# A transposed input that comes out of TensorE already normalised, in the first layer of a two-block transformer

## The chip, the cores and the metric

The kernel runs on one core of one Trainium2 chip. The metric is the device time of one execution in microseconds (us). Before the change it is 1310.2 us, the median of three runs (1309.93 to 1312.19). Lower is better.

## The reference, cut to what matters

Two transformer blocks run one behind the other on an input `x` of 256 tokens by 1024 features, in float32. The first block has a gated delta-net layer and a block-attention layer, each with an MLP. The second has four mixing branches, a cross-attention and a gated feed-forward. The change lies in the first few steps of the first layer:

```python
def rmsnorm(x, g):
    xf = x.astype(jnp.float32)
    y = xf * lax.rsqrt(jnp.mean(xf * xf, axis=-1, keepdims=True) + RMS_EPS)
    return (y * g.astype(jnp.float32)).astype(x.dtype)

def gated_deltanet(hn, w_in, ...):          # hn = rmsnorm(x, mix_norm_g[0])
    proj = hn @ w_in                         # q, k, v, z and 16 gate columns
    qkv = jax.nn.silu(causal_depthwise_conv(proj[..., :3 * DN_DIM], conv_w))
    ...
    beta = jax.nn.sigmoid(b_raw)             # from the gate columns
    g = -jnp.exp(a_log) * jax.nn.softplus(a_raw + dt_bias)
    o = chunk_gated_delta_rule(q, k, v, g, beta)   # needs a triangular solve
    ...

h = x
h = h + gated_deltanet(rmsnorm(h, mix_norm_g[0]), ...)
```

## The kernel before, in words

Everything is held transposed: features on the 128 partitions, the 256 tokens along the row. `x` is a tile of 8 such blocks, one for each 128 features. A float32 product is made from three products of half-precise parts. `split` writes a tile's high part on ScalarE and its low part on VectorE. The high and low parts of the normalised input are `xh` and `xl`, those of a weight `wh` and `wl`, and `mm3` adds the three products that matter. A weight comes from HBM in pieces of 512 KB (`wr`), fetched on SyncE's queue, four pieces deep.

The order of the instructions on each engine is set when the program is built, by a list scheduler that works from priorities (`high_priority`, `later`) and from `after`, which holds instructions back behind others. On the chip each engine works through its list in order and waits on semaphores.

The first layer goes as follows.

- `load_x` fetches `x` as two halves of 128 tokens (`xt`), transposes them on TensorE into four PSUM banks, and squares and sums the tokens on ScalarE (`token_rs`). That gives 1/rms of each token (`xrs`), put on a diagonal (`xdg`). A product of ones with the diagonals spreads 1/rms along a PSUM row (`p`).
- The transposed banks are copied to `x`. `normed` multiplies `x` by gain and row into a scratch tile `nrm` on VectorE, two blocks at a time, and splits it.
- `gates` makes the 16 gate columns (`ba`, transposed to `bat`) and from them `beta` and the log decay `gt`, through a string of tiny instructions (`sl_u` and the like). It needs two short rows from HBM, `alog` and `dtb`. `ea`, the exponential of `alog`, is the first to read one of them.
- `decays` turns `gt` into four decay tiles `m`. `project` makes k, q and v, a group of 512 columns at a time. Each group is 96 products of 128 columns into the two PSUM banks called `acc`. ScalarE empties them into `pad` and `cy`, VectorE adds three taps (12 instructions `cy` for a group), and ScalarE applies SiLU.
- `unit_keys` and `gram` give the matrices `A`. They travel through HBM (`ga`, `at`), and 31 steps of VectorE (`tmp`, `zt`) solve them. The result travels through HBM again (`gz`, `Z`), and TensorE goes on from `Z` ("Z stage" below). All 768 products of the eight groups (q, k and v, and the output gate `z`) stand ahead of the Z stage in TensorE's list.

## Time and profile before

| | |
|---|---|
| median of three runs | 1310.2 us |
| the profiled execution | 1310.08 us |
| its span in the trace | 1308.3 us |
| TensorE busy | 1261.0 us, 96% |
| VectorE busy | 867.1 us, 66% |
| ScalarE busy | 737.8 us, 56% |
| mean granted TensorE clock | 0.977 of full speed |

The span is the time between the first and the last instruction that the profiler saw. The profiled execution is 1.78 us longer than its span. A busy share is a mean over stages with different limits, so the start of the kernel has to be read by itself.

### The profile page before, as it was taken

The numbers are of one execution on the slowest core, as the hardware profiler recorded it, in microseconds if no ns is written. First come the engines' busy times: TensorE is split into PE (matmuls) and PEld (weight loads), VectorE is DVE, ScalarE is ACT, GpSimd is POOL, SyncE is SP. The second block draws the span as 40 slices with busy tenths as digits, with TensorE's granted clock in tenths as the row PEclk, the third lists the DMA queues.
The fourth block names the chain that finished last, engine by engine and source line by source line (L and its number), as shares of the span: only waits on it lengthen the run. The fifth ranks groups of instructions, "written<-read, shape, count | busy, mean of one in ns | idle before, by whom it ended". The sixth has DMA issues, their size and how long they took to land.

```text
span 1308.3 us, 23770 instructions
## 1 busy us (share of the span) xinstructions
PE 1261.0 (96%) x9674; PEld 1199.7 (92%) x9674; DVE 867.1 (66%) x1385; ACT 737.8 (56%) x1124; POOL 20.9 (2%) x68
## 2 busy tenths in 40 slices
PE   7997789999999999999999999999999998999998
PEld 6997688999999999999999987899999997999997
DVE  5799236644547666744546997998556685877775
ACT  5874536645546445755545644675447565656554
POOL 2010100000000000000000000000000000000000
PEclk8998689999999999999999999999999999999999
DMA  6454303666664744656652653446664654465652
GB/s 199 143 171 145 81 1 129 219 196 187 183 182 141 216 153 143 210 166 181 188 166 64 194 162 87 139 131 192 183 188 148 208 161 129 132 205 170 184 177 84
DMA packets 99633, 207.32 MB, mean 158 GB/s; under 512 B 9694, under 2 KB 12292, under 8 KB 99524
## 3 DMA queue, kind: packets, MB, share of 16 engines
q1 hardware_dynamic: 98114, 202.85, 50.7%
q0 software_dynamic: 928, 2.88, 0.8%
q8 instruction: 76, 1.25, 0.4%
q14 instruction: 33, 0.27, 0.1%
q10 hardware_dynamic: 482, 0.08, 0.0%
HBM read 204.21 MB, written 1.57 MB: 157 GB/s over the span
## 4 chain that ended last, share of the span: by engine, by line
PE 86%; DVE 6%; ACT 3%; issue 2%; DMA 2%; POOL 0%; DVEq 0%; SPq 0%; ACTq 0%; POOLq 0%
PE acc L53 53%; PE ps L53 32%; DVE wl L56 1%; ACT wh L76 1%; PE ps L603 1%; DVE cy L59 1%; DVE tmp L56 1%; PE ps L893 0%; DVE zt L56 0%; DVE sq L56 0%; DMA wr<-in_w_xkv_dram 0%; DMA xt<-in_x_dram 0%; DMA Z<-gz 0%; DMA gz<-zt 0%; DVE mx L879 0%
## 5 line engine op out<-in xcount | busy, mean ns | idle before, releaser
L56 DVE TENSOR_TENSOR wl<-wr,wh 128x1024 fp32r<-128x1024 f32 (+1 forms) x384 | 465.6, 1217 | 308.2 <-ACT wh L76 307.3
L76 ACT ACTIVATE wh<-wr 128x1024 fp32r<-128x1024 f32 (+1 forms) x384 | 402.3, 1052 | 394.3 <-PE acc L53 246.9
L53 PE MATMUL acc<-xh,wh 128*128 128x256 f32 (+1 forms) x1064 | 305.9, 288 | 7.8 <-DVE z L59 5.1
L53 PE MATMUL acc<-xh,wl 128*128 128x256 f32 (+1 forms) x1064 | 303.8, 286 | 3.5 <-DVE wl L56 3.5
L53 PE MATMUL acc<-xl,wh 128*128 128x256 f32 (+1 forms) x1064 | 304.4, 286 | 0.8 <-DVE xl L56 0.8
L53 PE MATMUL ps<-xh,wh 128*128 128x256 f32 (+1 forms) x872 | 248.5, 285 | 6.7 <-ACT xh L69 3.5
L53 PE MATMUL ps<-xl,wh 128*128 128x256 f32 (+1 forms) x872 | 248.2, 285 | 0.5 <-DVE xl L56 0.3
L53 PE MATMUL ps<-xh,wl 128*128 128x256 f32 (+1 forms) x872 | 248.0, 284 | 0.0
L53 PEld LDWEIGHTS acc<-xh,wh 128*128 128x128 f32 (+1 forms) x1064 | 204.4, 192 | 11.4 <-issue 6.5
L53 PEld LDWEIGHTS acc<-xh,wl 128*128 128x128 f32 (+1 forms) x1064 | 204.1, 192 | 6.0 <-DVE wl L56 3.7
L53 PEld LDWEIGHTS acc<-xl,wh 128*128 128x128 f32 (+1 forms) x1064 | 204.6, 192 | 3.2 <-issue 1.5
L53 PEld LDWEIGHTS ps<-xh,wh 128*128 128x128 f32 (+1 forms) x872 | 166.8, 191 | 8.4 <-ACT xh L69 3.9
L53 PEld LDWEIGHTS ps<-xl,wh 128*128 128x128 f32 (+1 forms) x872 | 166.9, 191 | 1.6 <-DVE xl L56 1.1
L53 PEld LDWEIGHTS ps<-xh,wl 128*128 128x128 f32 (+1 forms) x872 | 167.0, 192 | 0.3
L53 PE MATMUL acc<-hh,wh 128*128 128x256 f32 x512 | 144.6, 282 | 0.0
L53 PE MATMUL acc<-hh,wl 128*128 128x256 f32 x512 | 144.3, 282 | 0.0
L53 PE MATMUL acc<-hl,wh 128*128 128x256 f32 x512 | 144.2, 282 | 0.0
L53 PEld LDWEIGHTS acc<-hh,wl 128*128 128x128 f32 x512 | 97.3, 190 | 0.0
L53 PEld LDWEIGHTS acc<-hh,wh 128*128 128x128 f32 x512 | 97.2, 190 | 0.0
L53 PEld LDWEIGHTS acc<-hl,wh 128*128 128x128 f32 x512 | 97.1, 190 | 0.0
L59 DVE SCALAR_TENSOR_TENSOR yc<-cpad,vec_b,yc 128x256 f32<-128x256 f32 x120 | 51.6, 475 | 0.1
L59 DVE SCALAR_TENSOR_TENSOR fy<-pad,vec_b,fy 128x256 f32<-128x256 f32 x88 | 36.9, 478 | 0.1
(418 smaller groups left out, 1759.6 us busy)
## 6 DMA issues: line engine op xcount, KB each, us to landing
wr<-in_mlp_w_up_dram SPq DMA_DIRECT2D x64, 512.0 KB
wr<-in_mlp_w_down_dram SPq DMA_DIRECT2D x64, 512.0 KB
wr<-in_w_in_dram SPq DMA_DIRECT2D x44, 512.0 KB
wr<-in_w_up_dram SPq DMA_DIRECT2D x44, 512.0 KB
wr<-in_dn_w_in_dram SPq DMA_DIRECT2D x32, 512.0 KB
wr<-in_w_gate_dram SPq DMA_DIRECT2D x32, 512.0 KB
wr<-in_mb_w_in_dram SPq DMA_DIRECT2D x24, 512.0 KB
wr<-in_w_down_dram SPq DMA_DIRECT2D x22, 512.0 KB
```

Source lines behind the costliest of these rows:

```text
L53: return self.nc.tensor.matmul(out, lhsT=lhsT, rhs=rhs, start=start, stop=stop, skip_group_check=True)
L56: return (eng or self.nc.vector).tensor_tensor(out=out, in0=a, in1=b, op=op)
L59: self.nc.vector.scalar_tensor_tensor(out, a, s, b, op0=op0, op1=op1, **kw)
L76: a = self.nc.scalar.activation(hi, src, AF.Copy)
L603: nc.tensor.transpose(p[:, i * P:(i + 1) * P], zz[:, i, :], self.ident)
```

## The change

Both halves of `x` are now squared in two parts, one on VectorE (`stt` with a sum) and one on ScalarE. The diagonal of 1/rms is the right-hand operand of the products that transpose `xt`, so that the four PSUM banks hold the input transposed and normalised. `scaled` takes the high part (ScalarE) and the low part (VectorE) straight from PSUM, with the gain as the scale, one block of 256 at a time. `nrm` and the row `p` are gone. Eleven products of ones with themselves stand at TensorE's start in place of six. The plain transposes that `x` itself needs (it is added to the layer's output much later) come 200 priority steps later, out of `transposed_in`, with four copies on ScalarE. The first three 512 KB pieces of the weight are fetched ahead of the piece with the gate columns, which was first.

```diff
@@ load_x
-                banks = [self.ps() for _ in range(4)]
-                for i in range(6):
-                    self.mm(banks[i % 4][:, 0:P], self.ones, self.ones, True, True)
-                for c in range(2):
-                    for k in range(KD):
-                        o = (k % 2) * T + c * P
-                        tr = nc.tensor.transpose(banks[k // 2][:, o:o + P], xt[:, c, k * P:(k + 1) * P], self.ident)
-                dg = self.token_rs(xp, xt, "x", xp.tile([P, 2, D], F32, name="xsq"))
-                p = self.ps()
-                for c in range(2):
-                    row = self.mm(p[:, c * P:(c + 1) * P], self.ones, dg[:, c, :], True, True)
-                cp = nc.vector.tensor_copy(x[:, 0:2, :], self.pairs(banks[0]))
+                warm = self.ps()
+                for i in range(11):
+                    self.mm(warm[:, 0:P], self.ones, self.ones, True, True)
...
+                for c in range(2):
+                    if c:
+                        sq_after.enter_context(self.after(self.last_exp))
+                    u, v = ss[:, 2 * c:2 * c + 1], ss[:, 2 * c + 1:2 * c + 2]
+                    self.stt(sq[:, c, 0:half], xt[:, c, 0:half], 1.0, xt[:, c, 0:half], OP.mult, OP.mult, accum_out=u)
+                    self.act(sq[:, c, half:D], xt[:, c, half:D], AF.Square, accum_out=v)
+                    self.ts(u, u, 1.0 / D, EPS, OP.mult, OP.add)
+                    self.rsqrt_wide(rs[:, c:c + 1], v, D, u)
+                    last = self.ts(dg[:, c, :], self.ident, rs[:, c:c + 1], None, OP.mult)
...
+                for c in range(2):
+                    for k in range(KD):
+                        o = (k % 2) * T + c * P
+                        tr = self.mm(banks[k // 2][:, o:o + P], xt[:, c, k * P:(k + 1) * P], dg[:, c, :], True, True)
+                last = self.last_vec, self.last_exp, last
+                for i in range(4):
+                    with self.after(*last):
+                        if i < 3:
+                            self.ahead(W, 2 * i, 2, 1024, 512)
+                            last = self.last_split
+                        if i == 2:
+                            self.ahead(W, 0, 8, 4096, 16)
+                    o = self.pairs(banks[i])
+                    with self.after(*last):
+                        for j in range(2):
+                            last = self.scaled(xg, 2 * i + j, o[:, j, :], g[:, 2 * i + j:2 * i + j + 1])
+            with self.later(200), self.after(tr):
+                self.transposed_in(xt, None, lambda k, o: self.copy(x[:, k:k + 2, :], o))
-            with self.tc.high_priority():
-                for k in range(2, KD, 2):
-                    sc = self.copy(x[:, k:k + 2, :], self.pairs(banks[k // 2]))
-            last = sc, cp
-            for i in range(4):
-                with self.after(*last):
-                    last = self.normed(xp, xg, x, g, p[:, 0:T], range(2 * i, 2 * i + 2))
-                with self.after(*last):
-                    if i < 3:
-                        self.ahead(W, *((0, 8, 4096, 16) if i == 0 else (2 * i - 2, 2, 1024, 512)))
```

The scheduler then places many later instructions elsewhere. Three places matter. The first is the start of TensorE's list. `ps` and `acc` are PSUM banks, and `16x256` marks the gate columns. Before:

```order
L53 MATMUL ps<-tri 128x128 x6
L399 MATMUL ps<-ident,xt 128x128 x16
L53 MATMUL ps<-xdg,tri 128x128
L178 MATMUL ps<-ident,vrow_a_143 128x128
L178 MATMUL ps<-ident,vrow_a_144 128x9
L53 MATMUL ps<-xdg,tri 128x128
L53 MATMUL ps<-xh,wh 16x256
```

After the change:

```order
L53 MATMUL ps<-tri 128x128 x11
L177 MATMUL ps<-ident,vrow_a_113 128x128
L177 MATMUL ps<-ident,vrow_a_114 128x9
L53 MATMUL ps<-xdg,xt 128x128 x16
L53 MATMUL acc<-xh,wh 128x256
```

The gate columns no longer come first: their 24 products stand behind the 96 of the first k group. Further on, the products of `gt` (`decays`) stand behind 164 of the 768 `acc` products where they stood behind 116, and the last products of `gram` behind 286 where they stood behind 317. The plain transposes are spread through the first 170.

The second place is ScalarE's list, from the last high part of the input (`xh`) to the gate columns (`ba`). Before:

```order
L76 ACTIVATE xh<-nrm 128x512
L184 DMA alog<-in_dn_a_log_dram 128x8
L184 DMA dtb<-in_dn_dt_bias_dram 128x8
L76 ACTIVATE wh<-wr 128x1024
L72 ACTIVATE ba<-ps 16x256
L69 ACTIVATE ea<-alog 128x8
L76 ACTIVATE wh<-wr 128x1024
```

After the change:

```order
L68 ACTIVATE xh<-ps,vec_a 128x256
L183 DMA alog<-in_dn_a_log_dram 128x8
L183 DMA dtb<-in_dn_dt_bias_dram 128x8
L75 ACTIVATE wh<-wr 128x1024 x2
L68 ACTIVATE ea<-alog 128x8
L71 ACTIVATE pad<-acc 128x2x256
L68 ACTIVATE cy<-acc,vec_a 128x256 x2
L71 ACTIVATE pad<-acc 128x2x256
L68 ACTIVATE cy<-acc,vec_a 128x256 x2
L71 ACTIVATE x<-ps 128x512
L75 ACTIVATE wh<-wr 128x1024 x2
L71 ACTIVATE ba<-ps 16x256
```

`ea` moved from behind `ba` to a place ahead of it, and the emptying of the first k group, a copy to `x` and two high parts of weights now stand between the two.

The third place is VectorE's list from the last tiny steps of the gates to the second k group. Before:

```order
L59 SCALAR_TENSOR_TENSOR gt<-lp,ea 128x16
L59 SCALAR_TENSOR_TENSOR cy<-pad,vec_a,cy 128x256
L488 COPY gc<-ps 128x16
L59 SCALAR_TENSOR_TENSOR cy<-pad,vec_a,cy 128x256
...
L59 SCALAR_TENSOR_TENSOR cy<-pad,vec_a,cy 128x256 x2
L56 TENSOR_TENSOR wl<-wr,wh 128x1024 x2
L59 SCALAR_TENSOR_TENSOR cy<-pad,vec_a,cy 128x256 x12
L56 TENSOR_TENSOR wl<-wr,wh 128x1024 x3
L56 TENSOR_TENSOR k<-k,kr 128x512
```

After the change:

```order
L59 SCALAR_TENSOR_TENSOR gt<-lp,ea 128x16
L505 COPY gc<-ps 128x16
L56 TENSOR_TENSOR kdec<-ps,gc 128x8
L56 TENSOR_TENSOR beg<-beg,beta 128x8
L56 TENSOR_TENSOR m<-ps,gc 128x512 x4
L59 SCALAR_TENSOR_TENSOR cy<-pad,vec_a,cy 128x256 x12
L56 TENSOR_TENSOR wl<-wr,wh 128x1024 x2
L56 TENSOR_TENSOR k<-k,kr 128x512
```

All 12 `cy` of the first k group now stand ahead of `bat`, and so ahead of `gt`. Before, seven of them and two `wl` filled the stretch between `gt` and the second k group. Of the large `wl`, eleven stand ahead of `gt` where eight did. From the end of the solve (`zt`) on, the lists of all engines are the same as before. On GpSimd the clearing of `Z` (1 instruction, L501 before) moved from the start to behind the first `cy`.

## Rows read from the trace of the kernel before

**Rows 1.** The chain that ended last, in time: start us, length us, what.

```profile
131.24 0.20 DVE zt L56
...
144.82 1.10 PE ps L603 x4
```

**Rows 2.** Busy time by stage: start:end and length, then each engine (instructions), clock.

```profile
core 0: us, PE busy (x) PEld busy (x) DVE busy (x) ACT busy (x) POOL busy (x), PEclk, DMA share, GB/s
0.00:35.25 35.25, 27.58 (x176) 23.82 (x176) 22.11 (x52) 20.95 (x39) 6.59 (x13) 0.85 0.61 199
35.25:48.80 13.55, 13.43 (x115) 13.38 (x115) 7.99 (x17) 11.13 (x21) 0.21 (x2) 1.00 0.35 115
48.80:73.60 24.80, 24.69 (x185) 22.39 (x185) 22.55 (x47) 21.41 (x33) 0.32 (x3) 1.00 0.44 134
73.60:131.43 57.83, 49.08 (x375) 47.92 (x374) 54.99 (x129) 33.39 (x49) 4.43 (x11) 0.94 0.54 167
```

**Rows 3.** Busy time by stage again, around the fall of the clock.

```profile
7.60:9.60 2.00, 0.00 (x0) 0.00 (x0) 1.55 (x3) 2.00 (x7) 1.80 (x1) 0.87 1.04 376
9.60:19.20 9.60, 6.85 (x27) 4.61 (x28) 6.09 (x13) 3.78 (x9) 0.00 (x0) 0.50 0.28 85
```

**Rows 4.** Timeline of TensorE: start us, us, line, instruction, [idle before <-releaser].

```profile
1.05 2.93 PE L53 MATMUL ps<-tri 128*128 128x128 f32 x12 [1.05 <-DVE oeps L669]
...
6.43 1.09 PE L399 MATMUL ps<-ident,xt 128*128 128x128 f32 x8 [0.30 <-DMA xt<-in_x_dram]
...
62.37 1.07 PE L53 MATMUL ps<-k 128*128 128x128 f32 x8
```

**Rows 5.** Timeline of ScalarE: the same columns.

```profile
6.41 1.06 ACT L69 ACTIVATE xsq<-xt 128x1024 f32<-128x1024 f32 x1 [0.84 <-DMA xt<-in_x_dram]
...
7.46 0.46 ACT L69 ACTIVATE xrs<-xss,eps 128x1 f32<-128x1 f32 x2
...
21.54 0.35 ACTq L184 DMA_DIRECT2D alog<-in_dn_a_log_dram  x1
...
25.05 0.37 ACT L72 ACTIVATE ba<-ps 16x256 f32<-16x256 f32 x1 [1.49 <-PE ps L53]
25.83 0.21 ACT L69 ACTIVATE ea<-alog 128x8 f32<-128x8 f32 x1 [0.40 <-DMA alog<-in_dn_a_log_dram]
...
46.72 1.14 ACT L69 ACTIVATE sq<-k 128x512 f32<-128x512 f32 x2
47.76 0.58 ACT L72 ACTIVATE pad<-acc 128x512 f32<-128x512 f32 x1
48.24 0.82 ACT L69 ACTIVATE cy<-acc,vec_a 128x256 f32<-128x256 f32 x2
```

**Rows 6.** Groups of VectorE's instructions, 8 to 23.2 us: busy us, mean ns, idle.

```profile
L56 DVE TENSOR_TENSOR wl<-wr,wh 128x1024 fp32r<-128x1024 f32 x4 | 4.9, 1218 | 0.0
L59 DVE SCALAR_TENSOR_TENSOR nrm<-x,vec_a,ps 128x256 f32<-128x256 f32 x8 | 3.6, 476 | 1.4 <-PE ps L53 1.4
L56 DVE TENSOR_TENSOR xl<-nrm,xh 128x512 fp32r<-128x512 f32 x4 | 2.8, 689 | 2.1 <-ACT xh L76 2.1
L64 DVE TENSOR_SCALAR xdg<-ident,xrs 128x128 f32<-128x128 f32 x2 | 1.6, 1432 | 6.1 <-ACT xrs L69 6.1
```

**Rows 7.** Timeline of VectorE: the gates, then the second k group.

```profile
1.62 0.35 DVE L64 TENSOR_SCALAR tri<-jf,pf 128x128 f32<-128x128 f32 x1
...
25.81 0.19 DVE L474 COPY bat<-ps 128x32 f32<-128x32 f32 x1 [0.30 <-PE ps L473]
...
35.14 0.16 DVE L59 SCALAR_TENSOR_TENSOR gt<-lp,ea 128x16 f32<-128x16 f32 x1
...
48.80 4.84 DVE L59 SCALAR_TENSOR_TENSOR cy<-pad,vec_a,cy 128x256 f32<-128x256 f32 x12 [3.70 <-ACT cy L69]
```

**Rows 8.** Timeline of GpSimd.

```profile
7.67 1.80 POOL L501 MEMSET Z<- 128x2048 f32 x1 [2.02 <-issue]
```

**Rows 9.** The page's costliest groups: a weight's high part, busy us, mean ns, idle.

```profile
L76 ACT ACTIVATE wh<-wr 128x1024 fp32r<-128x1024 f32 (+1 forms) x384 | 402.3, 1052 | 394.3 <-PE acc L53 246.9
```

More of the change, by code (lines that the diff above doesn't have):

```diff
@@ L58, in stt @@
     def stt(self, out, a, s, b, op0, op1, **kw):
-        self.nc.vector.scalar_tensor_tensor(out, a, s, b, op0=op0, op1=op1, **kw)
+        return self.nc.vector.scalar_tensor_tensor(out, a, s, b, op0=op0, op1=op1, **kw)
     def ts(self, out, a, s1, s2, op0, op1=None, eng=None):
@@ L63, in ts @@
         if op1 is None:
-            e.tensor_scalar(out, a, s1, None, op0=op0)
-        else:
-            e.tensor_scalar(out, a, s1, s2, op0=op0, op1=op1)
+            return e.tensor_scalar(out, a, s1, None, op0=op0)
+        return e.tensor_scalar(out, a, s1, s2, op0=op0, op1=op1)
     def act(self, out, a, f, **kw):
@@ L132, in constants @@
         nc.vector.memset(self.ones, 1.0)
-        self.ts(self.tri[:, 0:P], jf, pf, None, OP.is_ge)
+        self.last_const = self.ts(self.tri[:, 0:P], jf, pf, None, OP.is_ge)
         self.eps = cp.tile([P, 1], F32, name="eps")
@@ L178, in vectors @@
             nc.tensor.transpose(pt[:, 0:n], rows[i][0:n, :], self.ident[0:n, 0:n])
-            self.copy(out[:, i * P:i * P + n], pt[:, 0:n])
+            self.last_vec = self.copy(out[:, i * P:i * P + n], pt[:, 0:n])
         return where
@@ L201, in weight @@
         nc.sync.dma_start(raw[:, 0:n].rearrange("p (k c) -> p k c", c=ncols), src)
-        self.split(hi[:, 0:n], lo[:, 0:n], raw[:, 0:n])
+        self.last_split = self.split(hi[:, 0:n], lo[:, 0:n], raw[:, 0:n])
         v = lambda t: t[:, 0:n].rearrange("p (k c) -> p k c", c=ncols)
@@ L282, in rsqrt_wide @@
                 ln()
-        self.act(out, out, AF.Exp, scale=-0.5)
+        self.last_exp = self.act(out, out, AF.Exp, scale=-0.5)
     def norm_row(self, sqs, n, tag="rsrow", bufs=2, after=None):
@@ L336, in scaled @@
         h, l = xg
-        self.act(h[:, k, :], src, AF.Copy, scale=g)
-        self.stt(l[:, k, :], src, g, h[:, k, :].bitcast(F32), OP.mult, OP.subtract)
+        i = self.act(h[:, k, :], src, AF.Copy, scale=g)
+        return i, self.stt(l[:, k, :], src, g, h[:, k, :].bitcast(F32), OP.mult, OP.subtract)
     def normed(self, pool, xg, x, g, row, ks=range(KD)):
@@ L390, in load_x @@
             xg = self.new_xg(0)
+            W = a["dn_w_in"][0]
+            half = D // 2
             with self.tc.high_priority():
-                banks = [self.ps() for _ in range(4)]
-                for i in range(6):
-                    self.mm(banks[i % 4][:, 0:P], self.ones, self.ones, True, True)
-                for c in range(2):
-                    for k in range(KD):
-                        o = (k % 2) * T + c * P
-                        tr = nc.tensor.transpose(banks[k // 2][:, o:o + P], xt[:, c, k * P:(k + 1) * P], self.ident)
-                dg = self.token_rs(xp, xt, "x", xp.tile([P, 2, D], F32, name="xsq"))
-                p = self.ps()
-                for c in range(2):
-                    row = self.mm(p[:, c * P:(c + 1) * P], self.ones, dg[:, c, :], True, True)
-                cp = nc.vector.tensor_copy(x[:, 0:2, :], self.pairs(banks[0]))
-            with self.after(tr):
+                warm = self.ps()
+                for i in range(11):
+                    self.mm(warm[:, 0:P], self.ones, self.ones, True, True)
                 self.vec = self.vectors([
@@ L412, in load_x @@
                 ], nc.scalar, "a", xp)
-            g = self.vec["mix_g"]
-            W = a["dn_w_in"][0]
-            with self.tc.high_priority():
-                for k in range(2, KD, 2):
-                    sc = self.copy(x[:, k:k + 2, :], self.pairs(banks[k // 2]))
-            last = sc, cp
-            for i in range(4):
-                with self.after(*last):
-                    last = self.normed(xp, xg, x, g, p[:, 0:T], range(2 * i, 2 * i + 2))
-                with self.after(*last):
-                    if i < 3:
-                        self.ahead(W, *((0, 8, 4096, 16) if i == 0 else (2 * i - 2, 2, 1024, 512)))
+                g = self.vec["mix_g"]
@@ new lines, in load_x @@
+                dg = xp.tile([P, 2, P], F32, name="xdg")
+                sq = xp.tile([P, 2, D], F32, name="xsq")
+                ss = xp.tile([P, 4], F32, name="xss")
+                rs = xp.tile([P, 2], F32, name="xrs")
+                sq_after = ExitStack()
+                sq_after.enter_context(self.after(self.last_const))
+                for c in range(2):
[7 more added lines that the diff above has]
+                    last = self.ts(dg[:, c, :], self.ident, rs[:, c:c + 1], None, OP.mult)
@@ new lines, in load_x @@
+                sq_after.close()
+                banks = [self.ps() for _ in range(4)]
+                for c in range(2):
[14 more added lines that the diff above has]
+                            last = self.scaled(xg, 2 * i + j, o[:, j, :], g[:, 2 * i + j:2 * i + j + 1])
```

## The prediction

> **What bounds the kernel now.** I read the chain that ended last first, because TensorE is busy for 96% of the span and the question is where it is not the bound. It is not the bound ahead of the Z stage. There the chain runs over VectorE: its last step of the solve starts at 131.24 us, two trips through HBM follow, and TensorE starts on `Z` at 144.82 [rows 1]. The order's lists are the same from the last `zt` on, so whatever the change does to that moment goes to the end of the kernel nearly one for one. The question is when VectorE ends its last `zt`, which is at 131.43 now.
>
> The busy time by stage says how full VectorE is up to there [rows 2]. To the end of `gt` it is busy for 22.11 of 35.25 us. From there to the second k group it is busy for 7.99 of 13.55, then for 22.55 of 24.80, and in the solve for 54.99 of 57.83. So it idles 13.1, 5.6, 2.3 and 2.8 us. The end of the solve is VectorE's work (107.6 us) and these idle times. The second one is a string of waits: VectorE stands for 3.70 us for ScalarE's `cy` at 48.80 [rows 7], and ScalarE comes to that only behind the decays, a table load and two `sq` [rows 5]. That string hangs on `gt`. So I follow two things: VectorE's work, and the moment of `gt` (35.14 now [rows 7]).
>
> **The change, part by part.**
>
> VectorE's work. Eight `nrm` go (3.6 us) and four `xl` of 512 (2.8). Eight `xl` of 256 come, at about the price of a `nrm` (0.476 each, 3.8 together), and two squares of 512, nearest to the old `xl` (0.689 each, 1.4). The two diagonals took 1.6 together, each 1.432 on the average [rows 6]. They ended with the clearing of `Z` on GpSimd, which ran from 7.67 to 9.47 [rows 8]. A like instruction took 0.35 alone [rows 7], so 0.7 for both now that the clearing has moved. Sum: about 2.1 us less work.
>
> The rows show VectorE held for as long as GpSimd's clearing ran. The Trainium skill, page "SBUF — State Buffer", section "SBUF: two separate sides", says that the two share a pair of ports as an exclusive lock, and that VectorE's instructions with two inputs in SBUF contend only with GpSimd instructions that read. By that rule the clearing costs nothing beside the `cy` where it stands now. From the rows alone it costs between 0 and its 1.80 us there. I take 0, as a `cy` is of another kind than the diagonals that the row shows held, and keep 1.80 for the range.
>
> The start of TensorE. The eleven warming products are 22 records of 0.24 us (12 took 2.93 [rows 4]), so they end near 6.3. They hide under the wait for `x`. The second half of `x` lands at 6.4 [rows 5]. VectorE's half of its squares takes 0.7, and the tiny instructions for both halves of the tokens stand behind it in its list. That is 7.3. Ln and Exp take 0.23 each (0.46 for two [rows 5]), the diagonal 0.35: the first products can start at 8.15. ScalarE squares its part for the second half only after that Exp (0.53, and some 0.2 to read the sum), so its diagonal is there near 9.35.
>
> The 16 transposing products are 32 records, where 16 transposes were 16 (8 in 1.09 [rows 4]). A record of this size takes 0.13 at the full clock (8 in 1.07) and 0.24 at half. The clock falls to its lower level, 0.5, at 9.1 before the change: the mean of 0.87 over 7.60 to 9.60 says so, after TensorE had ended at 7.52 [rows 3, 4]. The gap between the warming and the products is now about as long, 1.8 us. The first bank is full after 20 records: 10.8 at the full clock, 13.0 at half. I take the middle, 11.9.
>
> From there ScalarE has eight `xh` (0.41 each, like a `cy`: 0.82 for two [rows 5]), four and a bit `wh` (about 1.0 each [rows 9]), and two copies to `x` (0.5 each). That is 8.6. In each bank the second `xh` waits for the first `xl`, 0.5 each time: the built program has that wait, and I count 2 us for the four banks. The Trainium skill, "PSUM — Partial Sum Buffer", section "PSUM bank collisions raise a hardware error", says why: two engines may not read one bank at once. No row here shows that case, and by a free bank the sum would be 2 us shorter.
>
> ScalarE is then at 22.4 and issues the fetch of `alog`. Before, 4.3 us lay between its issue at 21.54 and `ea` at 25.83, which waited for it [rows 5]. Then `ea` was behind `ba`. Now it is ahead, and with it everything behind: `pad` and `cy` of the first k group, a copy, two `wh` and `ba`. Two `wh` fill the wait to 24.4. I take `ea` at 26.7 (24.4 if the row lands early). Emptying the first group, the copy and two `wh` are 5.0 (two `pad` of 0.48 to the next start, four `cy` of 0.36 to 0.41, 0.5, two times 1.0 [rows 5, 9]). So `ba` starts at 31.7, where it started at 25.05. `bat` follows 0.76 later [rows 5, 7], at 32.4. Four `wl` at 1.2 [rows 6] and a dozen tiny instructions of about 0.16 lie between `bat` and `gt`: 6.7. So `gt` comes at 39.1, 4.0 us later than now. TensorE has 48 more of k's products behind it by then (164 against 116), which does not help this string.
>
> From `gt` to the second group's `cy`: 13.7 us now. In ScalarE's list the two `sq` (1.04 to the next start) and one `wh` (1.0) have moved out, so 11.6: the `cy` start at 50.7, where they start at 48.80 [rows 5, 7]. VectorE waits longer here: the seven `cy` and two `wl` that filled the stretch are done before.
>
> From there to the last `A`: 24.80 now [rows 2]. VectorE has six `cy` and a `wl` less here and two `m` more. But the string SiLU, table load, four times Ln and Exp, `k`, `gram` sets the length, with `sq` late in it and 12 products between the last two `gram`. By VectorE alone it would be 22.5, by TensorE's list 24.3. I take 23.8. `A` ends at 74.5 where it ends at 73.60.
>
> From `A` to the last `zt`: 57.83 now [rows 2], and VectorE is full. The work that was not done before is now here: six `cy` (0.4 each) and one `wl` (1.2) more, two `m` (0.6) less, 2.4 net. That makes 60.2, and the last `zt` ends at 134.7. It is 3.3 us later than now. TensorE also has 31 products more behind the last `gram`, 3.7 us, which could hold VectorE's next `cy`; I count nothing for it, since TensorE idles later in this stage (49.08 busy of 57.83).
>
> The rest costs nothing. The plain transposes (some 2 us) fall where TensorE leads. Their copies are in the sums above. The fetch of the gate columns stands later on SyncE's queue, and its reader does too. The clearing of `Z` is needed only near 137.
>
> Sum, against the profiled execution: 1310.08 + 3.3 = **1313.4 us**. That execution lies 0.1 under the median. A measurement of this kernel can tell 0.2% from no change, 2.6 us.
>
> **The rivals.**
>
> *VectorE's work alone decides: faster.* If `gt` being late is absorbed, because VectorE has done 6.3 us more of other work by then, the idle times stay as they are and 2.1 to 2.8 us of work are gone: 1307.5. With the full clock at the start it would be 1306. For it: VectorE is full for 57.83 us [rows 2]. Against it: its list lets nothing pass the decays, and idle time there is what the moved `cy` filled. It decides if `gt` comes before about 35.5.
>
> *The two cancel: no change.* The clock stays up for the products (1.1 less), `alog` lands early (up to 2.3 less). Then `gt` comes near 36 and the sum is 1310.3. For it: the 4.3 us is a single reading, taken beside other transfers, and the clock's fall is near its edge. Against it: both would have to go this way.
>
> *The clock falls a second time: slower still.* TensorE waits some 4 us for the `sq` near 50 and again for `k` near 60. If the clock falls there as it did at 9.1, 40 to 80 products cost 0.1 more each, 4 us at the worst, of which TensorE's later idle time takes a part: 1317.
>
> **How the numbers follow.** I give the forecast 0.5, the faster rival 0.2, no change 0.2, the second fall 0.1. The lowest part of the forecast's own spread (1311.5 to 1316) lies within 2.6 us of the median; I count 0.12 of its chance as no change. So faster 0.21, same 0.31, slower 0.48. The range of 1306.5 to 1317.5 leaves out about half of the chance of the outer cases' tails, under 2 in 10.
>
> **What would show it.** `gt` near 39, `ba` near 32 with `ea` waiting for `alog` just before, VectorE idle for 8 us between `gt` and the second group's `cy`, the last `zt` near 134.7 and `Z` on TensorE near 148. If `gt` comes before 36, or the second group's `cy` before 48, the forecast is wrong at the string of the gates. If `gt` is late and `Z` is not, it is wrong in what VectorE can catch up.

## The result and the profile after

The changed kernel takes 1316.2 us, the median of five runs (1315.16 to 1320.42), where the kernel before takes 1310.2. The ratio is 1.0052, with a 95% interval of 1.0034 to 1.0071: it is slower by about 0.5%. Its profiled execution took 1319.55 us with a span of 1317.8, so it is one of the longer of the five, and its span is 9.5 us longer than before. A second profile of the same kernel (e1, 1317.73 us, span 1315.9) stands beside it below. A ratio here is not the quotient of the two medians, so the two can differ a little.

The chain that ended last, of the kernel after, up to the Z stage, in the columns of [rows 1]:

```profile
9.05 4.65 PE ps L53 x20
...
82.25 7.06 DMA wr<-in_dn_w_in_dram
...
123.78 5.17 DMA wr<-in_dn_w_out_dram
...
132.34 14.33 PE acc L53 x95
```

The last links before the Z stage are no longer VectorE's solve and the two trips through HBM. They are waits for a weight and TensorE's products. (`Z` reaches TensorE at 151.05, and the first copy of the Z stage, `X`, starts 2.01 us later, behind work of ScalarE that waited for those 95 products; before the change it started 1.12 us after `Z` came.) So I read the stages next. Busy time of the kernel after, cut at `gt`, the second k group's first `cy`, the last `A` and the last `zt`, as in [rows 2]:

```profile
0.00:41.52 41.52, 36.58 (x262) 35.13 (x262) 26.80 (x62) 23.89 (x46) 6.80 (x15) 0.92 0.64 202
41.52:53.09 11.57, 7.82 (x66) 7.65 (x66) 3.36 (x8) 9.14 (x18) 0.00 (x0) 0.98 0.21 63
53.09:76.70 23.61, 23.30 (x150) 20.12 (x151) 19.19 (x41) 18.68 (x30) 0.21 (x2) 0.86 0.36 112
76.70:138.19 61.49, 51.88 (x398) 50.29 (x397) 57.09 (x135) 35.71 (x52) 4.54 (x12) 0.92 0.54 159
```

Against [rows 2] the four stages are 6.3 longer, 2.0 shorter, 1.2 shorter and 3.7 longer. The last `A` ends at 76.70 (+3.1) and the last `zt` at 138.19 (+6.8). The first copy `X` of the Z stage starts at 153.06 on ScalarE, where it started at 145.94 (+7.1). The other 2.4 us come behind it. VectorE's busy time up to the last `zt` is 106.4 us, 1.2 less than the 107.6 before. Its idle time is 8.0 us longer: 1.6, 2.6, 2.2 and 1.6 in the four stages. In e1 the same differences are 1.75 to the last `A`, 3.66 in the solve, 0.16 to `X` and 2.0 behind.

The start, on TensorE's timeline:

```profile
6.70 0.30 PE L177 MATMUL ps<-ident,vrow_a 128*128 128x128 f32 x1 [1.09 <-DMA vrow_a<-in_mlp_norm_g_dram]
7.83 0.20 PE L177 MATMUL ps<-ident,vrow_a 9*128 9x9 f32 x1 [0.83 <-DMA vrow_a<-in_final_norm_g_dram]
9.05 6.75 PE L53 MATMUL ps<-xdg,xt 128*128 128x128 f32 x32 [1.02 <-DVE xdg L64]
```

The 32 records of the transposing products take 6.75 us. The granted clock was 0.59 from 8 to 10 us and 0.50 from 10 to 14, the lower level. ScalarE's timeline shows what followed, up to the gates:

```profile
13.72 0.47 ACT L68 ACTIVATE xh<-ps,vec_a 128x256 fp32r<-128x256 f32 x1 [2.93 <-PE ps L53]
14.75 0.47 ACT L68 ACTIVATE xh<-ps,vec_a 128x256 fp32r<-128x256 f32 x1 [0.55 <-DVE xl L59]
...
23.62 0.36 ACTq L183 DMA_DIRECT2D alog<-in_dn_a_log_dram  x1
...
26.88 1.06 ACT L75 ACTIVATE wh<-wr 128x1024 fp32r<-128x1024 f32 x1 [1.25 <-DMA wr<-in_dn_w_in_dram]
28.37 0.21 ACT L68 ACTIVATE ea<-alog 128x8 f32<-128x8 f32 x1 [0.43 <-DMA alog<-in_dn_a_log_dram]
...
33.23 0.35 ACT L71 ACTIVATE ba<-ps 16x256 f32<-16x256 f32 x1
...
44.31 1.29 ACT L68 ACTIVATE m<-m 128x512 f32<-128x512 f32 x2 [1.10 <-DVE m L56]
```

`ba` comes 8.2 us later than in [rows 5], and `ea` now stands ahead of it. The `m` of the decays starts at 44.31; before it is 38.03. VectorE's timeline for the same places ([rows 7]):

```profile
29.53 4.84 DVE L59 SCALAR_TENSOR_TENSOR cy<-pad,vec_a,cy 128x256 f32<-128x256 f32 x12 [0.33 <-ACT cy L68]
34.28 0.19 DVE L491 COPY bat<-ps 128x32 f32<-128x32 f32 x1
...
41.43 0.17 DVE L59 SCALAR_TENSOR_TENSOR gt<-lp,ea 128x16 f32<-128x16 f32 x1
...
53.09 4.84 DVE L59 SCALAR_TENSOR_TENSOR cy<-pad,vec_a,cy 128x256 f32<-128x256 f32 x12 [6.14 <-ACT cy L68]
```

In the solve, ScalarE stands for a weight that is still on its way:

```profile
89.40 1.06 ACT L75 ACTIVATE wh<-wr 128x1024 fp32r<-128x1024 f32 x1 [2.46 <-DMA wr<-in_dn_w_in_dram]
```

VectorE stands right behind it, and the first step of the solve (`tmp`, at 93.39) comes only after that:

```profile
91.40 2.07 DVE L59 SCALAR_TENSOR_TENSOR cy<-pad,vec_a,cy 128x256 f32<-128x256 f32 x5 [2.14 <-ACT cy L68]
```

The transfer took 7.06 us (the chain above). It was issued at 82.25, only after the `wl` at 81 had freed its buffer. GpSimd issued the two fetches of the solve's matrix (`at`) at 82.11, so both ran together, and these landed after 6.4 and 7.8 us (3.2 and 3.7 before).

### The profile page after: what moved, and what is told of

The parts are those of the page before. It is cut to its first block, busy times and chain, and to the rows that moved or that the text cites. A ratio compares the mean times of both kernels' runs of the same rounds, so it can differ in the third digit from the quotient of the medians.

```text
span 1317.8 us, 23861 instructions
## 1 busy us (share of the span) xinstructions
PE 1269.0 (96%) x9712; PEld 1208.7 (92%) x9712; DVE 866.2 (66%) x1386; ACT 739.0 (56%) x1129; POOL 20.9 (2%) x68
## 3 DMA queue, kind: packets, MB, share of 16 engines
q8 instruction: 76, 1.25, 0.4%
## 4 chain that ended last, share of the span: by engine, by line
PE 85%; ACT 5%; DVE 5%; DMA 3%; issue 2%; SPq 0%; ACTq 0%; DVEq 0%
PE acc L53 52%; PE ps L53 32%; ACT wh L75 1%; DVE wl L56 1%; DMA wr<-in_dn_w_in_dram 1%; PE ps L620 1%; PE ps L910 0%; DMA wr<-in_w_xkv_dram 0%; DVE sq L56 0%; DMA wr<-in_dn_w_out_dram 0%; DMA vrow_a<-in_final_norm_g_dram 0%; DMA alog<-in_dn_a_log_dram 0%; ACT m L68 0%; DVE mx L896 0%; DMA vrow_b<-in_norm_x_post_dram 0%
## 5 line engine op out<-in xcount | busy, mean ns | idle before, releaser
L56 DVE TENSOR_TENSOR wl<-wr,wh 128x1024 fp32r<-128x1024 f32 x384 | 466.3, 1219 | 309.7 <-ACT wh L75 309.0
L75 ACT ACTIVATE wh<-wr 128x1024 fp32r<-128x1024 f32 x384 | 402.5, 1053 | 399.8 <-PE acc L53 250.0
L59 DVE SCALAR_TENSOR_TENSOR cy<-pad,vec_a,cy 128x256 f32<-128x256 f32 x72 | 31.5, 486 | 8.9 <-ACT cy L68 8.9
```

What stands on the lines that cost most here:

```text
L56: return (eng or self.nc.vector).tensor_tensor(out=out, in0=a, in1=b, op=op)
L59: return self.nc.vector.scalar_tensor_tensor(out, a, s, b, op0=op0, op1=op1, **kw)
L75: a = self.nc.scalar.activation(hi, src, AF.Copy)
```

## The experiments

The time of each kernel stands beside runs of the kernel before on the same chip, whose medians were 1310.3 to 1310.8. Times in the table come from each kernel's one profile, in us: the start of `gt`, of ScalarE's first `m` and of `X`, the end of the last `A`, and then the solve (from there to the end of the last `zt`) and what lies behind `X` to the end of the span.

| kernel | `gt` | first `m` | last `A` ends | solve | `X` | behind `X` | median of runs |
|---|---|---|---|---|---|---|---|
| before | 35.14 | 38.03 | 73.60 | 57.83 | 145.94 | 1162.4 | 1310.2 |
| after | 41.43 | 44.31 | 76.70 | 61.49 | 153.06 | 1164.7 | 1316.2 |
| e1 | 40.62 | 43.49 | 75.35 | 61.49 | 151.51 | 1164.4 | 1316.1 |
| e2 | 37.14 | 40.03 | 71.76 | 58.75 | 145.19 | 1162.8 | 1313.9 |
| e3 | 37.95 | 40.83 | 72.61 | 58.78 | 146.06 | 1164.3 | 1311.8 |
| e4 | 36.30 | 39.49 | 73.88 | 57.91 | 145.88 | 1160.8 | 1310.5 |
| e5 | 35.16 | 40.53 | 76.28 | 57.87 | 148.75 | 1165.2 | 1314.1 |
| e6 | 35.69 | 38.87 | 73.27 | 57.86 | 145.52 | 1162.9 | 1311.5 |
| e7 | 34.79 | 37.98 | 72.39 | 57.62 | 145.57 | 1161.9 | 1309.6 |
| e8 | 29.16 | 40.98 | 75.35 | 57.98 | 147.57 | 1165.2 | 1313.5 |
| e9 | 34.01 | 37.26 | 73.03 | 56.63 | 144.15 | 1162.4 | 1308.6 |
| e10 | 34.34 | 37.64 | 69.36 | 59.33 | 143.82 | 1161.7 | 1307.8 |
| e11 | 34.68 | 37.59 | 71.21 | 59.81 | 146.08 | 1164.8 | 1313.3 |
| e12 | 34.37 | 37.27 | 72.86 | 58.74 | 146.21 | 1164.6 | 1312.2 |

One profile can lie some us from the median of its kernel (e2's is 1309.76 us, 4.2 under it), so small differences between rows of the table are not differences between kernels.

**e1, the changed kernel once more.** 

> The changed kernel once more, unedited, beside the three that follow, to have its time on the same chip and a second profile. Every theory: 1315 to 1320 us. What the profile is asked for: whether the two late stalls that the prediction did not have (about 7 us of waiting for a weight's transfer near 82 us, TensorE at its lower clock near 128 to 138) are there again. If they are there in a run of about 1316, they are part of the 6 us; if only in one of about 1320, they belong to the upper end of the spread alone.

Measured: 1316.1, ratio 1.0045 (1.0031 to 1.0059). The wait for the weight is there again (2.19 us at 87.77). So are the solve's length and TensorE's lower clock at the end of it (from 125.8 to 136.1 us; in the first profile from 127.8 to 138.1).

**e2, the two short rows early.** 

> The changed kernel, with the two small rows (alog and dtb) fetched right behind the vectors at the start. The prediction's step (ea waits for alog and holds pad, cy and ba behind it; up to 2.3 us of the string) says: gt from 41.4 to 39, time 1314. The rival reading of the trace after the change: ea waited for only 0.43 us, and ba stands behind pad, cy, a copy and two wh in any case, so gt comes at 40.5 to 41 and the time stays at 1315 to 1317.

```diff
                 g = self.vec["mix_g"]
+                self.alog = self.bcast_rows(a["dn_a_log"][0], 8, "alog", nc.scalar)
+                self.dtb = self.bcast_rows(a["dn_dt_bias"][0], 8, "dtb", nc.scalar)
...
-            with self.after(*last):
-                self.alog = self.bcast_rows(a["dn_a_log"][0], 8, "alog", nc.scalar)
-                self.dtb = self.bcast_rows(a["dn_dt_bias"][0], 8, "dtb", nc.scalar)
```

Measured: 1313.9, ratio 1.0029 (1.0018 to 1.0041), and `gt` at 37.14. The time is the one that the prediction's step asks for. But its profile is the fastest of its runs (1309.76 us): the clock did not fall at 8 to 16 us in it, so its early rows are those of a lucky start. And the built list changed in more places than `ea`'s: by the trace the products of `gt` stand behind 153 of k's products (164 in the changed kernel) and the last `gram` behind 272 (286). So it doesn't isolate that wait.

**e3, the gates' weight first.** 

> The changed kernel, with the 16 gate columns of the weight fetched and split ahead of the three big pieces, as before the change. If the late weight makes the gates late: ba near 27, gt near 36, time 1310 to 1312. If what holds the gates' products is something else (they still stand behind 96 of k's products in TensorE's list, as the built program has it): gt after 40, time 1315 to 1317.

```diff
-                        if i < 3:
+                        if i == 0:
+                            self.ahead(W, 0, 8, 4096, 16)
+                        if i < 3:
                             self.ahead(W, 2 * i, 2, 1024, 512)
                             last = self.last_split
-                        if i == 2:
-                            self.ahead(W, 0, 8, 4096, 16)
```

Measured: 1311.8, ratio 1.0008 (0.9998 to 1.0017). Neither theory has it right. `ba` is late still (31.03) and the gates' products are still behind 96 of k's, as the second said. Yet most of the loss is gone: `gt` at 37.95, the last `A` 2.7 us earlier than in e1, and the solve 2.7 us shorter, without the long wait for a weight. Further on in TensorE's list, the products of `gt` and the last `gram` moved to the places that they have in e2 (153 and 272).

**e4, the gates ahead of the plain transposes.** 

> The changed kernel, with the gates' 24 products and the two transposes of ba written ahead of the plain transposes of x (which wait for them), everything else as it is. The plain transposes then no longer take PSUM banks ahead of the gates, and the gates' products stand among the first 38 to 67 of k's products. Theory (the plain transposes, cheap by themselves, push the gates' string back): ba near 27, gt near 36, DVE idle ahead of the second k group's cy back to about 4 us, last zt near 132, time 1309 to 1312. Rival (the loss is the slow start: products at the lower clock, xh and xl taking turns in a bank, xl of 256 in place of nrm): gt may be early, but the time stays at 1314 to 1316.

```diff
+            ba = dp.tile([16, T], F32, name="ba")
+            self.lin(W, KD, [(4096, 16)], self.reader(xg), lambda c, o: self.copy(ba, o[:, 0, :]), tag="ps")
+            pb = self.pb = self.ps()
+            for c in range(2):
+                gtr = nc.tensor.transpose(pb[:, c * 16:c * 16 + 16], ba[:, c * P:(c + 1) * P], self.ident[0:16, 0:16])
-            with self.later(200), self.after(tr):
+            with self.later(200), self.after(gtr):
                 self.transposed_in(xt, None, lambda k, o: self.copy(x[:, k:k + 2, :], o))
```

(The same lines leave `gates`.) Measured: 1310.5, ratio 0.9997 (0.9987 to 1.0007): the loss is gone. ScalarE's timeline of e4 has `ba` where it was before:

```profile
25.02 0.37 ACT L71 ACTIVATE ba<-ps 16x256 f32<-16x256 f32 x1
```

So writing the gates ahead of the plain transposes is enough to take the loss away. By the traces the gates' products stand behind 38 to 60 of k's products here, where all of them stand behind 96 in the changed kernel, and the 16 plain transposes behind 108 to 124, where they stand behind 32 to 100 (the section on the change has them up to 170). It does not show that the place of the plain transposes alone makes the change slow: e3 leaves the gates and the plain transposes where they were in TensorE's list, and most of the 6 us is gone there too. What e3 and e4 share is that the gates come earlier. The slow start of the changed kernel is still in e4 (first `xh` at 12.82; 13.72 in the changed kernel, 12.32 in e1) and costs nothing that shows in the time.

**e5, all three.** 

> e4 with the gate columns fetched first (as in e3) and alog and dtb fetched at the start (as in e2). In e4 the string of the gates still waited for dtb (0.47 us) and for ea's alog (0.37). Theory that the string of the gates alone sets the time: gt from 36.3 to 34, A end 72.5, last zt near 130.5, time 1308 to 1310. Rival: from gt before about 36 on VectorE's own work or TensorE's list sets the end of A, and the time stays at 1310 to 1311.

(Edits of e2, e3 and e4 together.) Measured: 1314.1, ratio 1.0031 (1.0020 to 1.0042). Both theories were wrong: `gt` is earlier by 1.1 us than in e4 and the kernel 3.7 us slower. ScalarE's timeline of e5 shows one reason:

```profile
40.03 0.60 ACT L71 ACTIVATE x<-ps 128x512 f32<-128x512 f32 x1 [2.90 <-PE ps L373]
40.53 1.29 ACT L68 ACTIVATE m<-m 128x512 f32<-128x512 f32 x2
```

A copy to `x` stands ahead of `m` in ScalarE's list and waits for a plain transpose that TensorE has behind k's products. Between `gt` and `m` lie 5.4 us here, and 2.9 before. Two `wl` that VectorE has ahead of its own `m` (2.35 us) lie in the same time, so the 2.90 us are not all lost to the transpose. And of the 7.3 us between the profiles of e5 and e4, 2.4 lie ahead of the last `A` and 4.4 behind `X`.

**e6, the parameter rows between the products.** 

> e4 with the two transposes of the parameter rows moved from ahead of the products to between the products of the two halves, and ScalarE's two vec_a copies behind its second Exp. In the changed kernel ScalarE's first Ln stood behind the second vec_a, which waited for a late small fetch (first diagonal at 8.71 where 7.9 was forecast). Theory that this wait costs the start: first diagonal at 7.9, first xh from 12.8 to 12.0, time 0.8 us less than e4. Rival (weights' transfers and VectorE set the pace up to the gates): first xh earlier, ba and gt as in e4, time as e4.

```diff
                 for c in range(2):
+                    if c:
+                        with self.after(tr, self.last_exp):
+                            self.turn_vec()
                     for k in range(KD):
```

(`turn_vec` is the loop of transposes and copies that stood at the end of `vectors`.) Measured: 1311.5, ratio 1.0003 (0.9992 to 1.0015), on top of e4. The first diagonal starts at 7.53 (8.71 in the changed kernel), the first `xh` at 12.47, and the time doesn't tell it from e4.

**e7, more warming.** 

> e6 with 18 warming products in place of 11, so that TensorE is busy up to its first product with the diagonal. Theory that the lower clock is what the transposing products cost (32 records took 6.75 us at half clock, some 4 at full): granted clock 1.0 from 8 to 16 us, first xh near 11, first banks 1.5 to 2 us earlier than e6, and the time 1 to 2 us less if ScalarE's start goes through to gt. Rival: ScalarE then waits for the weights' transfers (1.33 us for wr at 26.7 in e4) and the time stays within 0.5 us of e6.

```diff
-                for i in range(11):
+                for i in range(18):
                     self.mm(warm[:, 0:P], self.ones, self.ones, True, True)
```

Measured: 1309.6, ratio 0.9995 (0.9983 to 1.0007), on top of e6. Busy time by stage of e7, at the start:

```profile
8.00:10.00 2.00, 2.00 (x18) 1.83 (x17) 0.29 (x1) 0.54 (x3) 0.00 (x0) 1.00 0.99 290
10.00:12.00 2.00, 2.00 (x18) 1.98 (x19) 0.67 (x1) 1.66 (x4) 0.00 (x0) 1.00 0.10 9
```

The clock stays at its upper level, each half's 16 records take 2.05 us (2.94 and 2.56 in e6), and the first `xh` starts at 11.18. The last `A` is 0.9 us earlier than in e6. The intervals of the two times overlap, so the 1.9 us between the medians are not shown to be real.

**e8, xh and xl in different banks.** 

> e4 with the blocks of x taken from PSUM in the order 0 2 1 3, 4 6 5 7, so that ScalarE's xh and VectorE's xl are in different banks, where they took turns in one. The prediction counted 2 us for the turns (0.5 in each bank). If that holds: no waits of xh for xl at 13.8 and 17.0, last xh from 22.9 to 21, gt up to 2 us earlier, time 1308.5 to 1309.5. Rival: the turns lay beside waits for the weights' transfers, gt may come earlier by the order of VectorE's list, but the end of A and the time stay as in e4.

```diff
+                turns = {1: (0, 2, 1, 3), 3: (4, 6, 5, 7)}
...
-                        for j in range(2):
-                            last = self.scaled(xg, 2 * i + j, o[:, j, :], g[:, 2 * i + j:2 * i + j + 1])
+                    for k in turns.get(i, ()):
+                        with self.after(*last):
+                            last = self.scaled(xg, k, self.pairs(banks[k // 2])[:, k % 2, :], g[:, k:k + 1])
```

Measured: 1313.5, ratio 1.0027 (1.0017 to 1.0036), on top of e4. ScalarE's timeline of e8:

```profile
12.55 2.10 ACT L68 ACTIVATE xh<-ps,vec_a 128x256 fp32r<-128x256 f32 x4 [1.32 <-PE ps L53]
...
40.48 0.60 ACT L71 ACTIVATE x<-ps 128x512 f32<-128x512 f32 x1 [2.50 <-PE ps L373]
40.98 1.29 ACT L68 ACTIVATE m<-m 128x512 f32<-128x512 f32 x2
```

Four `xh` now run without a wait, the last `xh` starts at 18.72 where e4 has it at 22.86, and `gt` comes at 29.16. Nothing of the 7.1 us by which `gt` is earlier than in e4 is left at `m`. TensorE comes to the products of `gt` only at 35.35, as k's products stand ahead of them in its list:

```profile
35.35 0.73 PE L53 MATMUL ps<-gt,tri 128*128 128x8 f32 x6
```

That is 6.2 us behind `gt` (0.2 in e4). Then comes the same wait of ScalarE for a plain transpose ahead of `m`. Of the 6.1 us between the profiles of e8 and e4, 4.4 lie behind `X`.

**e9, the plain transposes behind the grams.** 

> e7 with the plain transposes of x and their four copies moved on, behind the last gram (x's buffer is kept until then, in the place that z takes later). In e5 and e8, where the gates came early, ScalarE stood 2.90 and 2.50 us for a plain transpose, with the decays' m behind it in its list. Theory that the plain transposes hold ScalarE ahead of the decays: m and the first sq about 0.7 us (the wait for a bank in e4) to 2 us (the four copies) earlier than in e7, A end from 72.4 to 71, time 1308 to 1309.5. Rival: in e7 the m wait for gt, gc and VectorE, not for the copies; the first sq and A end as in e7, and the copies cost their 2 us in the solve instead: 1309.5 to 1311.

```diff
-            with self.later(200), self.after(gtr):
-                self.transposed_in(xt, None, lambda k, o: self.copy(x[:, k:k + 2, :], o))
+            self.plain = lambda: self.transposed_in(xt, None, lambda k, o: self.copy(x[:, k:k + 2, :], o))
...
             behind = [self.last_exp]
+            with self.later(200), self.after(self.last_gram):
+                self.plain()
```

Measured: 1308.6, ratio 0.9987 (0.9978 to 0.9996), on top of e7. It is faster than the kernel before. The `m` is 0.7 us earlier than in e7, as expected. The last `A` is not: it comes 0.6 us later.

**e10, the gates early as well.** 

> e9 with the gate columns fetched first and alog and dtb at the start, as in e5. e5 had gt 1.1 us earlier than e4 and still was 3.7 us slower. Theory that it was the plain transposes on ScalarE and TensorE ahead of the decays: without them gt at 33.5, first sq at 48, and with TensorE's list at 235 of k's products ahead of the first gram (256 in e7) A end near 69, last zt near 127.5, time 1305 to 1307.5. Rival (something else in e5, as TensorE's list, which had A1 wait 2.18 us): A end after 72 and no gain on e9.

(Edits of e2 and e3 on e9.) Measured: 1307.8, ratio 0.9984 (0.9975 to 0.9993). Busy time by stage of e10, cut at the same four places:

```profile
0.00:34.50 34.50, 31.20 (x239) 29.39 (x239) 22.72 (x60) 20.28 (x41) 6.71 (x14) 1.00 0.71 218
34.50:47.37 12.87, 10.35 (x87) 10.18 (x87) 7.45 (x13) 11.15 (x20) 0.10 (x1) 1.00 0.51 155
47.37:69.36 21.99, 21.04 (x144) 18.09 (x145) 17.57 (x39) 17.13 (x28) 0.21 (x2) 0.92 0.29 86
69.36:128.69 59.33, 53.27 (x419) 51.91 (x418) 57.29 (x136) 38.62 (x58) 4.55 (x12) 0.94 0.55 171
```

What made e5 slow now helps: the last `A` ends 4.2 us earlier than before the change [rows 2] and the last `zt` 2.7 us earlier. The time is 0.3 us above the expected range. `Z` reaches TensorE 4.1 us earlier than before (140.68 against 144.82), but `X` starts only 2.1 us earlier: it is now 3.1 us behind `Z`, where ScalarE is still at work for the output gate `z`.

**e11, one part alone: the gates' weight third, before the change.** 

> The kernel before, with the gate columns fetched third as the change does, nothing else. If the late gate weight alone pushes the string of the gates back: ba after 28, gt after 37, time 1312 to 1314. If it takes the plain transposes as well (without them the built list has the gates' products among the first 47 to 59 of k's products, as against 96 in the changed kernel): gt within 1.5 us of 35.1, time 1309 to 1311.

```diff
                     if i < 3:
-                        self.ahead(W, *((0, 8, 4096, 16) if i == 0 else (2 * i - 2, 2, 1024, 512)))
+                        self.ahead(W, 2 * i, 2, 1024, 512)
+                    if i == 2:
+                        self.ahead(W, 0, 8, 4096, 16)
```

Measured: 1313.3, ratio 1.0025 (1.0014 to 1.0036). `gt` came at 34.68, so the late weight alone does not push the gates back (with the plain transposes at the start, their products stand behind 47 to 55 of k's). The kernel lost 2.5 us all the same, and in the profile none of it lies ahead of the Z stage: `X` is 0.1 us later than before and the part behind it 2.5 us longer.

**e12, a small delay ahead of the Z stage.** 

> The kernel before, with two multiplications of zt by 1.0 behind the last step of the solve (0.3 to 0.7 us each), nothing else; the lists of all engines are otherwise the same. In the profiles so far the part from the Z stage's first X to the end is 1160.8 to 1162.9 us where X starts by 145.94, and 1164.3 to 1165.2 where it starts at 146.06 or later (granted clock below 1.0 at 216 to 224, where it otherwise stays up). Theory of a step: X at 146.6 to 147.4, clock below 1.0 near 216, the part behind X 1164 or more, time 1312.5 to 1314.5. Rival (the part behind X has another cause, as the lists of the changed kernel): X later by the same 0.7 to 1.4, the part behind X 1162 to 1163, time 1311 to 1312.

```diff
                     self.tt(zt[:, 0:n, j + 1:32], zt[:, 0:n, j + 1:32], u, OP.subtract)
+                for _ in range(2):
+                    self.ts(zt, zt, 1.0, None, OP.mult)
```

Measured: 1312.2, ratio 1.0007 (0.9996 to 1.0018). The two instructions take 0.89 us together. This run's start was 0.8 us faster than the one of before (`gt` at 34.37), so `X` starts only 0.27 us later. Busy time by stage behind the Z stage, of the kernel before:

```profile
212.00:216.00 4.00, 1.61 (x12) 1.20 (x11) 3.08 (x5) 1.57 (x2) 0.00 (x0) 1.00 0.47 132
216.00:220.00 4.00, 4.00 (x36) 4.00 (x36) 3.19 (x10) 2.00 (x5) 0.00 (x0) 1.00 1.00 323
```

and of e12:

```profile
212.00:216.00 4.00, 2.45 (x19) 2.11 (x18) 2.80 (x3) 2.51 (x4) 0.00 (x0) 1.00 0.27 67
216.00:220.00 4.00, 3.16 (x15) 3.10 (x15) 2.53 (x8) 0.00 (x0) 0.00 (x0) 0.54 0.82 260
220.00:224.00 4.00, 4.00 (x24) 4.00 (x23) 2.35 (x6) 2.70 (x6) 0.00 (x0) 0.61 0.55 204
```

TensorE has the same gap of some 2.4 us in both. In e12 the clock is at its lower level behind it, before it is not. The profile has 2.2 us more behind `X`, as the theory said. The ratio over twelve runs (0.9 us, from -0.5 to 2.4) is that of the rival, and its interval reaches into the theory's range. So the step is shown in the profile, and how often it comes in a run is open. That a later `X` is its cause is not shown: `X` is 0.27 us later here, and e2 has the step with `X` at 145.19 (last section).

## Why the prediction was right, and where its sum was short

**The direction and the string were right.** Slower was the forecast. `gt` was to be late behind ScalarE's start and behind `ea`, VectorE was to idle for 8 us up to the second k group, and the solve was to take longer. `ea`, `ba`, `bat` and `gt` came in that order, VectorE idled for 8.2 of 11.57 us, and from `gt` to the `cy` were 11.66 us (forecast 11.6). Three experiments bear out that the late gates are what makes the change slow: each of e2, e3 and e4 brings `gt` forward in its own way, and each takes part or all of the loss away. The size is another matter. The forecast of 1313.4 was 2.8 us short of the median. That lies just above the forecast's own spread (1311.5 to 1316) and within the range, but both profiled executions (1319.55 and 1317.73) lie outside it. So the range was met with little to spare.

**The start was up to 2 us worse.** The first products came at 9.05 (forecast 8.15): ScalarE's first Ln stood behind two `vec_a` copies, and the second of those waited for a late parameter row. The clock fell, at the worse of the two bounds: the first `xh` came at 13.72, where the middle of the bounds was 11.9. The late start goes through to `ba` (33.23, forecast 31.7); 0.3 us more are lost from there to `bat` and 0.5 to `gt`, which misses 39.1 by 2.3. In e1 the first `xh` comes at 12.32 and `gt` still misses by 1.5, so the start is not all of it. Whether the start reaches the end once the gates are ahead is open: e6 moved the first `xh` by 0.35 us only, and e7, which moved it by 1.3 us more, had its last `A` 0.9 us earlier and no gain that the runs show.

**The turns in a bank** took about what was forecast, though not in even parts: two waits of `xh` for `xl`, 0.55 us at 14.75 and 1.32 at 17.86, where the sum has four of 0.5. The Trainium skill, page "PSUM — Partial Sum Buffer", section "PSUM bank collisions raise a hardware error", says that two engines may not read a bank at once; the waits of `xh` for `xl` in the rows of the changed kernel, which the program itself puts there, agree. But the step "by a free bank the sum would be 2 us shorter" is not borne out. In e8 the turns are gone and the last `xh` is 4.1 us earlier than in e4, and the time is 3.0 us longer. On the changed kernel itself it was not tried.

**`alog`** was a smaller part than the 2.3 us given to it. `ea` started 4.75 us after the row's issue (forecast 4.3), but ScalarE had other work in that time and a wait of 1.25 us for a weight, and `ea` waited for 0.43. With the rows fetched early (e2) `ba` comes 1.8 us earlier than in e1, and 1.0 of that is there at the first `xh` already.

**"The rest costs nothing" did not hold as it was argued.** The plain transposes are cheap in TensorE's time, and they fall where TensorE leads. Their price is in the lists. In the changed kernel the gates' products stand behind 96 of k's products. The sum had the time of these lists (`ba` at 31.7), but not a word on what made them so. With the gates written ahead of the plain transposes (e4) their products stand behind 38 to 60, and the loss of 6 us is gone; with the gates' weight fetched first (e3) most of it is gone, though the gates stay behind 96. Where the gates are early and the plain transposes still ahead of the decays (e5, e8), ScalarE waits 2.5 to 2.9 us for one with `m` behind. With the transposes behind the grams (e9, e10) the kernel is faster than before. That they take PSUM banks from the gates is only argued from the built lists; no run shows it.

**`gt` was the wrong moment to follow.** What goes on to the second k group is ScalarE's first `m`. Here `m` follows `gt` by 2.9 us before and after, so it made no difference for the forecast, but in e8 `gt` at 29.16 is worth nothing: TensorE reads it 6.2 us later, and ScalarE waits then.

**The solve was to be 2.4 us longer** and is 3.66 longer in both profiles. The prediction counted work, and the work is 2.1 us more; VectorE's idle time is 1.56 us more, and the sum had left it as it was. It did not see that with eleven `cy` ahead of three `wl` in VectorE's list, a weight's buffer would come free late and the transfer of the next one would run into the fetch of `at`. ScalarE's wait of 2.46 us (2.19 in e1) is followed by VectorE's of 2.14; e3 and e4 have no such wait ahead of the first step, and solves of 58.78 and 57.91. The order of VectorE's list is not all of the cause: e3 has twelve `cy` ahead of two `wl`, its next weight was issued at 78.56, 0.43 us behind the first fetch (0.14 in the changed kernel), and it was there in time.

**"To the end nearly one for one"** left out 2.0 to 2.4 us behind `X`, though all lists are the same there. That is the largest single term that was missing in e1 (4.3 us in all: 0.9 up to the last `A`, 1.3 in the solve, 0.2 to `X` and 2.0 behind). The granted clock is the reason that the rows show. Behind the wait for `Z` it came back to its upper level 32.8 us behind `X` (30.4 before; 32.3 in e1), and it fell once more 70 us behind `X` (0.65 from 224 to 228 us), which it did not before.

**The rivals.** GpSimd's clearing of `Z` beside VectorE's `cy` costs nothing: it ran from 32.41 to 34.22, in the middle of the twelve `cy` at 29.53, which took 4.84 us as before [rows 7]. By the rule of the Trainium skill (page "SBUF — State Buffer", section "SBUF: two separate sides") they don't contend, and the trace agrees. VectorE's saved work (forecast 2.1 us, 1.2 in the profile) is no rival to the loss: e4 has the same new instructions and is as fast as before. The clock did fall a second time, as the third rival has it. TensorE stood 3.83 us for ScalarE's `cy` up to 53.40, and the clock was at its lower level from 52.73 to 59.56 (0.66 from 50 to 60). The kernel before and e4 have no fall there, and e10, the fastest, has one half as long (0.79 from 48 to 56). It can have cost TensorE some 3 us at most (an estimate: half of the 6.16 us that TensorE was busy in it). VectorE shows little of it: its wait for TensorE ahead of the `A` at 68.33 is 1.34 us (0.81 before), and the stage took 23.61 us where the forecast, without a fall, had 23.8. So that rival's 1317 came close to the median for a reason that is mostly not its own; no run takes this fall away alone. (Its sum is off, too: 80 products at 0.1 us are 8 us and not 4.)

## What to carry to other kernels

Work that is cheap on its engine and "can be done later" still stands somewhere in an in-order list, on every engine that handles it. Ask what stands behind its copies and what its scratch buffers hold up, and put it behind the string that matters by a dependency, not by a priority alone. Judge a string by the last instruction before its consumer, not by one in its middle: a value that comes 7 us earlier (e8) is worth nothing when the next engine's list holds something else in front. And before crediting a delay one for one to the end, look whether the clock's steps further on come at the same places.

## What was not expected of the hardware

**A step behind the Z stage.** The 14 profiles fall into two groups there, although what stands in the lists is nearly the same. In six (before, e4, e6, e7, e9, e10) the granted clock, which is at its lower level behind the wait for `Z`, is back at the upper one 30.0 to 31.5 us behind `X`, and it does not fall again near 70 us behind `X`. In eight (the changed kernel twice, e2, e3, e5, e8, and e11 and e12, which are edits of the kernel before) it is back 32.3 to 32.8 us behind `X`, and 70 us behind `X` it falls again for 3.4 or 6.8 us. Here are the two us from 30.5 us behind `X`, in the columns of [rows 2], for the kernel before, e2 and e12:

```profile
176.44:178.44 2.00, 2.00 (x20) 2.00 (x19) 1.38 (x2) 0.00 (x0) 0.00 (x0) 1.00 0.00 0
175.69:177.69 2.00, 2.00 (x11) 2.00 (x11) 0.69 (x1) 0.00 (x0) 0.00 (x0) 0.50 0.00 0
176.71:178.71 2.00, 2.00 (x11) 2.00 (x11) 0.69 (x1) 0.00 (x0) 0.00 (x0) 0.50 0.00 0
```

A block of 155 products further on shows what is lost by then. In the chains of the same three profiles it starts 91.0, 93.0 and 94.2 us behind `X` (in the six 90.7 to 91.5, in the eight 93.0 to 94.3):

```profile
236.90 18.93 PE ps L53 x155
238.15 18.93 PE ps L53 x155
240.43 18.93 PE ps L53 x155
```

The medians of the six kernels are 1307.8 to 1311.5 and those of the eight 1311.8 to 1316.2. So a good part of what tells the experiments apart may be this step and not the string ahead of it. The moment of `X` does not decide: e2 has the step with `X` at 145.19, and e6, e7 and the kernel before don't have it with `X` at 145.52 to 145.94. Of the part from `X` to the end (1160.8 to 1162.9 us in the six and e2, 1164.3 to 1165.2 in the others) some comes from later places, as e2 shows. Why the clock comes back later, and why the same gap of TensorE is then followed by the lower level, stays open.

**Two transfers at once.** A weight of 512 KB and the two fetches of `at` took 7.06 and 6.4 to 7.8 us when the weight was issued 0.14 us behind the first fetch. In e3 it was issued 0.43 us behind, and the fetches took 3.6 and 5.7. In e4, where the next weight was issued 2.8 us behind the first fetch, they took 3.6 and 4.0.
